# Hybrid streaming encoder step on one Trainium2 core: the SSM's Toeplitz matrix through DRAM, the weight ring filled in two halves, the GELU quarters at later steps

## The chip, the cores and the metric

The kernel runs on one core of one Trainium2 chip. The metric is the time of one execution on the device in microseconds (us), lower being better. One execution was also recorded by the hardware profiler; all rows below come from it. The engines are named as in the profile: PE is TensorE's matmul, PEld its weight load, DVE is VectorE, ACT is ScalarE, POOL is GpSimd, SP is SyncE, which issues nearly all transfers (SPq is its queue of instructions).

## The reference, cut to what matters

One layer of a streaming encoder on 1024 prompt and 64 sample positions, 1088 columns in all, model width 1024, everything in fp32.

```
xn = rmsnorm(h, gain);  z = xn @ w_in            # q, k, v, zA, u, zB, gA, gB in one product
attn = sliding-window attention(q, k, v)         # 64-query blocks, sinks, partial rotary
y    = Re(C h) + D u,  h = A h + B u             # SSM: 32 groups of 16 channels, 64 complex states
s    = gelu(y);  s = s * sigmoid(s @ w_glu)
ya = (attn * silu(zA)) @ w_o_attn;  ys = (s * silu(zB)) @ w_o_ssm
h = h + (sigmoid(gA) * ya + sigmoid(gB) * ys) @ w_out
h = h + sigmoid(h @ w_pg) * (p @ w_pp);  y = rmsnorm(h, final_gain)
```

## The kernel before, in words

Activations lie transposed: 128 channels on the partitions, 1088 columns along the free axis, as 43 slots (`S.alloc`) of one such tile each, and four more in the tile `quad`. A free slot is handed out first in, first out, so a transfer into a slot waits for whoever read it last. Every fp32 product is made of three matmuls, L259 to L261 (`mm3`): weight and operand are each split into a rounded high part and the rest, and low times high, high times low and high times high are summed. A split (`split_to`, `hl_split`) is one ACT copy (L1134) and one DVE subtraction (L162).

**Steps.** The program is written as a long row of matmul groups. Each group calls `pump()` twice (once in the stages called `seven`), which counts a clock of steps and runs whatever was planned for that step with `at(step, f)`. So the tables `ROUND_AT`, `OUT_AT`, `BACK_AT`, `RING_AT`, `X_AT` say beside which matmuls the side work is written. The framework then schedules all of it, so an instruction can stand on its engine somewhat ahead of or behind the place where it was written. Each engine runs its own row in order, and each waits on semaphores for what it reads or overwrites.

**SSM rounds.** The SSM runs in eight rounds r of four groups. `s_wb` (step `ROUND_AT[r]`) builds a 128x64 tile `m` and then the Toeplitz matrix `t4` of the round by eight transfers, L736, each of which copies a part of `m`, shifted down by 16 rows per i, from SBUF to SBUF in runs of 16 floats (64 bytes). `s_state` (L765 and a chain of DVE and POOL operations) computes the states, `s_state2` finishes them. `s_out` (step `OUT_AT[r]`) multiplies: L815 uses the Toeplitz matrix, L816 the states; ACT evicts with L817, and L820 writes the result to `y_dram`. `tt_` holds two Toeplitz tiles, used in turn; both are zeroed once by POOL (L719), and the transfers write only the triangle that isn't zero.

**GELU.** When two rounds have written a quarter q of y, `s_back` (step `BACK_AT[q]`, L825) reads it back into `quad`; five steps later `s_gelu` squares it on ACT (L831), then `s_gelu2` makes the polynomial (DVE L835, and one multiplication L182 that `ENG["gelu"]` gives to DVE, DVE, POOL in turn) and a tanh on ACT (L837), and `s_gelu3` the last multiplication on DVE (L168 `quad<-s,quad`). The result is read only by `z_split`, far into the stage `seven(4)`, which begins at step 196.

**The ring.** From step 144 on, weights come through a ring of four pieces: `rload` transfers a raw weight (L173 on SP), `make` splits one half of it into the next piece. `ring_start`, at step `RING_AT` = 142, takes four slots and makes four pieces at once; `RAWS` = 3 is how many raw weights may lie ready.

**The stretch around the change.** Steps 120 to 143 are the product with `w_o_attn` (m = 4 to 7, stage OA here, evicted by ACT L173 into `quad`). Steps 144 to 167 are four gate units m = 4 to 7 of 24 products each (stage M here): blocks of 384, 384 and 320 columns, evicted by DVE (L162 `s<-bank`), then tanh (L1313). Meanwhile the operand sums for the stages `seven` are built from `x` (`x_load` L1274, `x_sums` L1278, the POOL rows of 544 columns, splits of 544 columns). From step 168 on `seven(2)` and then `seven(4)` run Strassen-like products: each piece of the ring serves two sub-blocks of 272 columns, and the bank of one product is copied out by ACT (L173) before the next product may add to it.

Of the kernel before, what the change touches and what calls it, by code (L numbers as in the profile page):

```python
# [12 lines left out]
F32 = mybir.dt.float32  # L13
# [7 lines left out]
P = 128  # L21
# [14 lines left out]
OFF = dict(load=-6, e=-5, wb=0, rot=-1, cf=0, st2=1, gelu=5)  # L36

ENG = dict(tab="VG", e="V", cf="VG", rot="VG", r8="GGGV", unrot="VG", rotadd="VVG", rope="VVVG", ropeadd="GGV", ropec="VG",
           gelu="VVG", norm="VG", w="V", gate="VG", glu="GGGV", mg="VVG", pa="V", h="V", acc="V",
           y="VVVG", z="V", ph="VVG", xs="G", ws="V", rs="VG", ms="V", hq="G", zz="GV", tcp="AV")  # L40
BACK_AT = (152, 158, 164, 170)
ROUND_AT = (32, 40, 50, 73, 86, 103, 121, 140)
OUT_AT = (41, 49, 60, 81, 98, 113, 137, 150)
SLOT = 1096
# [3 lines left out]
BLK2 = [(0, 416), (416, 416), (832, 256)]  # L48
HT = T // 2
RAWS = 3  # L50
RING_AT = 142
RING = 4
X_AT = (148, 151, 154, 158)

# [81 lines left out]
def emit(nc, tc, a, es, dbg=None):  # L136
# [5 lines left out]
    dp = pool(name="dr", bufs=1, space=bass.MemoryType.DRAM)  # L142

    S = Slots(sp, NSLOT)
# [3 lines left out]
    pp_dram = dp.tile([8, P, T], F32, name="pp_dram")  # L148
    pa_dram = dp.tile([8, P, T], F32, name="pa_dram")
    gb_dram = dp.tile([8, P, T], F32, name="gb_dram")  # L150
    zb_dram = dp.tile([4, P, T], F32, name="zb_dram")

    V, G, A, PE, DMA = nc.vector, nc.gpsimd, nc.scalar, nc.tensor, nc.sync
# [85 lines left out]
    def at(i, f, *args):  # L239
        plan.setdefault(i, []).append((f, args))  # L240
# [7 lines left out]
    def later(n, f, *args):  # L248
        at(clock["i"] + n, f, *args)
# [37 lines left out]
    warm = small([P, 256], "warm")  # L287
# [8 lines left out]
    c, cn = BLK[0]  # L296
# [115 lines left out]
    V = Recorder()  # L412
# [227 lines left out]
    V, vtt, stt = V_, vtt_, stt_  # L640
# [71 lines left out]
    def s_wb(r):  # L712

        half(r, "wb")
        sq, e, wb = hget(r, "sq", "e", "wb")
        if r == 0:
            tt_.extend([S.ahalf(), S.ahalf()])
            for x in tt_:
                G.memset(S.hap(x)[:, :512], 0.0)  # L719
        t = S.hap(tt_[r % 2])  # L720
        b = bank[5]
        for x in range(4):
            c = 256 * (x % 2) + P * (x // 2)
            PE.transpose(b[:, P * x:P * x + P], e[:, c:c + P], ident)
        A.activation(wb[:, :512], b, AF.Copy)
        b = bank[7]
        for j in range(2):
            o = b[:, 32 * j:32 * j + 32]
            PE.matmul(o, e[:, P * j:P * j + P], sq[:, SQ_CBR + 32 * j:SQ_CBR + 32 * j + 32], start=True, stop=False)
            PE.matmul(o, e[:, 256 + P * j:256 + P * j + P], sq[:, SQ_NCI + 32 * j:SQ_NCI + 32 * j + 32],  # L730
                      start=False, stop=True)
        m = sq[:, SQ_M:SQ_M + 64]
        vtt(m, b[:, :64], sq[:, SQ_D:SQ_D + 64], ADD)
        t4 = t[:, :512].rearrange("p (g i c) -> p g i c", g=4, i=8)
        for i in range(8):
            DMA.dma_start(t4[0:16 * (i + 1), :, i], m[16 * (7 - i):P].rearrange("p (g c) -> p g c", g=4))  # L736
        hfree(r, "e")

    def s_cf(r):
# [13 lines left out]
    rw, tt_ = {}, []  # L753
# [97 lines left out]
    for r, b in enumerate(ROUND_AT):  # L851
# [5 lines left out]
        if r % 2:  # L857
            q = r // 2
            b = max(BACK_AT[q], OUT_AT[r])
            at(b, s_back, q)  # L860
# [14 lines left out]
    for m in (2, 3):  # L875
        uq[m] = S.alloc()
        w = wget()
# [238 lines left out]
    for mp in range(2):  # L1116
        ts = [gate_unit() for _ in range(2)]
        w = wget()
# [33 lines left out]
    raws, pieces = [], []  # L1152
# [35 lines left out]
    ring = []  # L1188
    rst_ = {}
    ri = {"load": 0, "made": 0, "get": 0}  # L1190

    def rload(n, most=99):
        while ri["load"] < min(n, len(raws)) and len(rst_) < most:
            i = ri["load"]
            rst_[i] = S.alloc()
            first(DMA.dma_start, S.ap(rst_[i])[:, :1024], raws[i])
            ri["load"] += 1

    def make():

        j = ri["made"]
        ri["made"] += 1
        if j >= len(pieces):
            return
        name, i, x, done = pieces[j]
        top = max([i] + ([x] if name[0] == "S" else []))
        rload(top + 1)
        hl = hl_of(ring[j % RING], 512)
        A11, A12 = (S.ap(rst_[i])[:, 512 * y:512 * y + 512] for y in range(2))
        if name[0] == "S":  # L1210
            A21, A22 = (S.ap(rst_[x])[:, 512 * y:512 * y + 512] for y in range(2))
        s1, s2 = (S.ap(ring[-1])[:, 512 * y:512 * y + 512] for y in range(2))
        if name == "S2":
            first(ett, "ws", s1, A21, A22, ADD)
            first(ett, "ws", s2, s1, A11, SUB)
        elif name == "S3":
            first(ett, "ws", A11, A11, A21, SUB)
        elif name == "S4":
            first(ett, "ws", s2, A12, s2, SUB)
        first(hl_split, hl, (A11, A12)[x] if name == "half" else {"S1": s1, "S3": A11}.get(name, s2))  # L1220
        for y in done:
            S.free(rst_.pop(y))
        rload(top + 2, RAWS)

    def pget(n):
        c = ri["get"]
# [14 lines left out]
        pump()  # L1241
        return ps

    def ring_start():
        ring.extend(S.alloc() for _ in range(RING))
        for _ in range(RING):
            make()

    at(RING_AT, ring_start)
    OA = []  # L1250
    for m in range(4, 8):
        if m % 2 == 0:
            w = wget()
# [163 lines left out]
            S.free(GB[x, r])  # L1417

    for k in range(4):
        later(k, x_t1, k)  # L1420
    get = tile_of(ZB)
    seven(2, XP, XSUB, quarters(get, HT, scaled(get), z_late))
    zb, pin = [], []
# [70 lines left out]
    mg, pa = {}, {}  # L1494
# [117 lines left out]
    acc = S.ap(S.alloc())  # L1612
# [35 lines left out]
    for i, (blks, m) in enumerate(steps):  # L1648
        w = pget(2)
        pp_load(i + 1)  # L1650
        pp = S.ap(pq[i])
        for ci in blks:
# [6 lines left out]
            h = h2(m, ci)  # L1659
# [146 lines left out]
```

## Time and profile before

| what | value |
|---|---|
| median of three runs | 881.44 us (879.93 to 883.45) |
| the profiled execution, its own time | 882.6 us |
| its span, first to last instruction | 880.8 us |
| PE busy | 839.0 us (95%) |
| DVE busy | 634.3 us (72%) |
| ACT busy | 359.4 us (41%) |
| POOL busy | 234.4 us (27%) |

PE is busy 95% of the span, so what can be won is the 5% in which it waits and the stretches in which it runs at the lower of its two clock levels. In the profile's 40 slices PE is full nearly everywhere; the slices that are not lie at the start, at 160 to 180 us, at 380 to 400 us, at 420 to 460 us, near 600 and 665 us and at the end. A granted clock (PEclk) of 1.00 is 2.4 GHz, of 0.50 is 1.2 GHz.

### The profile page before, as it was taken

The page shows a single profiled execution, that of the slowest core. Times are in us where ns is not written, and L with a number is a line of the kernel's source. Part 1 is how long each engine was busy: PE and PEld are TensorE (multiplying, and loading weights), DVE is VectorE, ACT ScalarE, POOL GpSimd, SP SyncE. Part 2 cuts the span into 40 slices and gives each one's busy share as a digit, 9 for nine tenths or more (in the row PEclk, how much of TensorE's full clock was granted, in tenths as well). Part 3 has the DMA queues.
Part 4 walks back from the last instruction along what each step waited for, and adds up shares of the span by engine and source line. Part 5 has one row for each costly group of instructions (what it writes and reads, how often), then busy time and mean ns, then how long its engine had stood idle before and what let it go on. Part 6 is the DMA issues. An engine that isn't in the chain of part 4 may idle for free.

```text
span 880.8 us, 14634 instructions
## 1 busy us (share of the span) xinstructions
PE 839.0 (95%) x5571; PEld 801.2 (91%) x5571; DVE 634.3 (72%) x1222; ACT 359.4 (41%) x743; POOL 234.4 (27%) x232
## 2 busy tenths in 40 slices
PE   7999999899999999969979999999999999999994
PEld 6999999677779999969979999999999999999994
DVE  6897699666679758646788766778996556655476
ACT  7312211455543121235444434544447325444552
POOL 4178464111142323127311010140000322100052
PEclk9999999999999999979999999999999999999997
DMA  8431022201002232352342522287254620632124
GB/s 324 153 121 51 21 56 69 72 25 47 12 1 76 55 121 74 93 183 101 125 151 80 191 100 76 91 307 279 76 183 178 238 76 25 225 123 89 60 97 174
DMA packets 59719, 101.26 MB, mean 115 GB/s; under 512 B 23936, under 2 KB 38912, under 8 KB 59648
## 3 DMA queue, kind: packets, MB, share of 16 engines
q1 hardware_dynamic: 59504, 100.31, 33.3%
q8 instruction: 44, 0.72, 0.3%
q14 instruction: 27, 0.22, 0.1%
q10 hardware_dynamic: 144, 0.00, 0.0%
HBM read 74.31 MB, written 24.81 MB: 113 GB/s over the span
## 4 chain that ended last, share of the span: by engine, by line
PE 67%; DVE 14%; DMA 5%; issue 5%; POOL 5%; ACT 3%; SPq 1%; POOLq 0%; DVEq 0%; ACTq 0%
PE bank L259 20%; PE bank L261 19%; PE bank L260 19%; DVE s L162 4%; POOL s L182 4%; DVE s L182 2%; DVE s L168 2%; PE bank L1001 2%; PE bank L1055 2%; PE bank L1043 2%; DVE s L206 1%; DMA quad<-y_dram 1%; POOL quad L182 1%; DMA s<-p 1%; ACT s L204 1%
## 5 line engine op out<-in xcount | busy, mean ns | idle before, releaser
L259 PE MATMUL bank<-s,s 128*128 128x384 f32 (+4 forms) x1568 | 500.5, 320 | 16.5 <-DVE s L168 5.3
L260 PE MATMUL bank<-s,s 128*128 128x384 f32 (+4 forms) x1568 | 494.8, 316 | 0.0
L261 PE MATMUL bank<-s,s 128*128 128x384 f32 (+4 forms) x1568 | 494.6, 316 | 0.0
L259 PEld LDWEIGHTS bank<-s,s 128*128 128x128 f32 x1568 | 297.2, 190 | 25.6 <-issue 6.9
L260 PEld LDWEIGHTS bank<-s,s 128*128 128x128 f32 x1568 | 297.3, 190 | 2.2 <-issue 1.4
L261 PEld LDWEIGHTS bank<-s,s 128*128 128x128 f32 x1568 | 297.3, 190 | 0.6 <-issue 0.2
L162 DVE TENSOR_TENSOR s<-s,s 128x512 fp32r<-128x512 f32 (+3 forms) x172 | 133.2, 786 | 60.0 <-ACT s L1134 54.1
L182 POOL TENSOR_TENSOR s<-s,s 128x272 f32<-128x272 f32 (+5 forms) x73 | 94.3, 1296 | 216.8 <-DVE s L162 95.0
L1134 ACT ACTIVATE s<-s 128x512 fp32r<-128x512 f32 (+1 forms) x150 | 92.9, 631 | 63.0 <-PE bank L261 40.7
L182 DVE TENSOR_TENSOR s<-s,s 128x256 f32<-128x256 f32 (+5 forms) x148 | 93.6, 644 | 15.6 <-ACT s L1667 7.6
L173 ACT ACTIVATE s<-bank 128x272 f32<-128x272 f32 (+4 forms) x111 | 46.5, 428 | 112.4 <-PE bank L261 97.7
L168 DVE SCALAR_TENSOR_TENSOR s<-s,s 128x416 f32<-128x416 f32 (+5 forms) x66 | 44.8, 693 | 37.0 <-ACT s L173 29.4
L162 DVE TENSOR_TENSOR s<-bank,s 128x272 f32<-128x272 f32 (+3 forms) x105 | 46.2, 462 | 32.8 <-PE bank L730 14.4
L204 ACT ACTIVATE s<-s 128x1024 fp32r<-128x1024 f32 (+5 forms) x38 | 35.3, 935 | 69.0 <-PE bank L261 53.1
L182 POOL TENSOR_TENSOR quad<-quad,s 128x272 f32<-128x272 f32 (+1 forms) x14 | 18.0, 1296 | 110.4 <-DMA quad<-x 90.6
L182 POOL TENSOR_TENSOR s<-s 128x256 f32<-128x256 f32 (+3 forms) x26 | 25.2, 973 | 68.3 <-DVE s L162 24.8
L206 DVE TENSOR_TENSOR s<-s,s 128x1024 fp32r<-128x1024 f32 (+3 forms) x30 | 34.5, 1161 | 4.6 <-ACT s L204 4.6
L1010 ACT ACTIVATE s<-bank,at 128x192 f32<-128x192 f32 (+2 forms) x68 | 27.0, 409 | 23.9 <-DVE at L168 23.9
L165 POOL TENSOR_TENSOR rst<-rsw,mhalf 128x3 f32<-128x3 f32 (+4 forms) x7 | 6.0, 872 | 111.8 <-DVE rsw L363 111.8
L1134 ACT ACTIVATE s<-quad 128x544 fp32r<-128x544 f32 x36 | 23.1, 656 | 28.4 <-DVE quad L182 27.8
L182 POOL TENSOR_TENSOR s<-s,at 128x768 f32<-128x768 f32 (+1 forms) x8 | 14.8, 1853 | 52.2 <-DVE at L1019 35.9
L162 DVE TENSOR_TENSOR s<-quad,s 128x544 fp32r<-128x544 f32 x36 | 26.0, 744 | 1.2 <-ACT s L1134 1.2
(145 smaller groups left out, 776.7 us busy)
## 6 DMA issues: line engine op xcount, KB each, us to landing
s<-w_in SPq DMA_DIRECT2D x32, 512.0 KB
s<-x SPq DMA_DIRECT2D x19, 544.0 KB
s<-w_pg SPq DMA_DIRECT2D x16, 512.0 KB
pa_dram<-s SPq DMA_DIRECT2D x8, 544.0 KB
gb_dram<-s SPq DMA_DIRECT2D x8, 544.0 KB
quad<-gb_dram SPq DMA_DIRECT2D x8, 544.0 KB
s<-pa_dram SPq DMA_DIRECT2D x8, 544.0 KB
pp_dram<-quad SPq DMA_DIRECT2D x8, 544.0 KB
```

The source lines that it names most:

```text
L162: V.tensor_tensor(o, x, y, op)
L168: V.scalar_tensor_tensor(o, x, s, y, op0, op1)
L173: f(*x, **k)
L182: (nc.gpsimd if eng(key) == "G" else nc.vector).tensor_tensor(o, x, y, op)
L204: A.activation(f32r(h), x, AF.Copy, scale=1.0 if scale is None else scale)
L206: (G if on == "G" else V).tensor_tensor(f32r(l), x, h, SUB)
L259: PE.matmul(ps, f32r(wh), f32r(xl), start=first, stop=False, **k)
L260: PE.matmul(ps, f32r(wlo), f32r(xh), start=False, stop=False, **k)
L261: PE.matmul(ps, f32r(wh), f32r(xh), start=False, stop=last, **k)
L1001: PE.matmul(o, q, KTR[rows, 64 * n + 64 - nk:64 * n + 64], start=True, stop=True)
L1010: A.activation(pe[:, 64 + x * nk:64 + (x + 1) * nk], bank[3 + kv][:, jp * nk:(jp + 1) * nk], AF.Exp, bias=nm[:, x:x + 1], scale=0.125, acc ...
L1134: A.activation(f32r(hl[0]), raw, AF.Copy)
```

## The change

Three things change.

1. The Toeplitz matrix. `s_wb` no longer copies in eight parts from SBUF to SBUF. It writes `m` (128x64) to a DRAM tile `t_dram[r % 2]` of 240 rows, whose last 112 rows are zeroed once from `warm` at round 0, and reads it back with one transfer whose source is shifted by -16 rows per i: 128 partitions x 4 groups x 8 shifts, 4096 runs of 64 bytes. The eight transfers moved 4 x (16 + 32 + ... + 128) = 2304 such runs. The two POOL zeroings go.
2. The ring. `ring_start` runs twice, at steps 136 and 143, with two slots and two pieces each; up to step 143 only one raw weight may lie ready, then three.
3. The GELU. `BACK_AT` moves from 152, 158, 164, 170 to 176, 186, 196, 206, and all four multiplications L182 go to DVE. The four splits `x_t1` come one step later.

```diff
-           gelu="VVG", norm="VG", w="V", gate="VG", glu="GGGV", mg="VVG", pa="V", h="V", acc="V",
+           gelu="V", norm="VG", w="V", gate="VG", glu="GGGV", mg="VVG", pa="V", h="V", acc="V",
-BACK_AT = (152, 158, 164, 170)
+BACK_AT = (176, 186, 196, 206)
...
-RING_AT = 142
+RING_AT = (136, 143)
...
+    t_dram = dp.tile([2, 240, 64], F32, name="t_dram")
...
         if r == 0:
             tt_.extend([S.ahalf(), S.ahalf()])
-            for x in tt_:
-                G.memset(S.hap(x)[:, :512], 0.0)
+            for x in range(2):
+                DMA.dma_start(t_dram[x, P:], warm[:112, :64])
...
         t4 = t[:, :512].rearrange("p (g i c) -> p g i c", g=4, i=8)
-        for i in range(8):
-            DMA.dma_start(t4[0:16 * (i + 1), :, i], m[16 * (7 - i):P].rearrange("p (g c) -> p g c", g=4))
+        m_dram = t_dram[r % 2]
+        DMA.dma_start(m_dram[0:P], m)
+        rows = bass.AP(m_dram.tensor, m_dram.offset + 112 * 64, [[64, P], [16, 4], [-1024, 8], [1, 16]])
+        DMA.dma_start(t4, rows)
         hfree(r, "e")
...
-        rload(top + 2, RAWS)
+        rload(top + 2, ri["raws"])
...
-    def ring_start():
-        ring.extend(S.alloc() for _ in range(RING))
-        for _ in range(RING):
-            make()
-
-    at(RING_AT, ring_start)
+    def ring_start(raws_):
+        ring.extend(S.alloc() for _ in range(2))
+        ri["raws"] = raws_
+        make()
+        make()
+
+    at(RING_AT[0], ring_start, 1)
+    at(RING_AT[1], ring_start, RAWS)
...
     for k in range(4):
-        later(k, x_t1, k)
+        later(k + 1, x_t1, k)
```

**How instructions move.** In the changed file lines behind the new one are numbered one to five higher: L259 to L261 become L260 to L262, L815 and L816 become L818 and L819, L736 becomes L737 (write) and L739 (read), L173 becomes L174, L831 and L837 become L834 and L840. Names such as `s17_134_2664` are a slot and its user; `bank2_66` is a PSUM bank.

TensorE at the end of OA, before. `s17_134` holds the last weight of OA, `s42_168` the ring's first piece:

```order
L260 MATMUL bank2_66<-s17_134_2664,s3_4_82 128x320
L261 MATMUL bank2_66<-s17_134_2664,s2_3_81 128x320
L815 MATMUL bank5_69<-s10_74_1109,s9_75_1110 128x136
L815 MATMUL bank6_70<-s10_74_1109,s9_75_1110 128x136
L816 MATMUL bank5_69<-s11_167_3566,s5_160_3348 128x136
L815 MATMUL bank5_69<-s10_74_1109,s9_75_1110 128x136
L816 MATMUL bank5_69<-s11_167_3566,s5_160_3348 128x136
L816 MATMUL bank6_70<-s11_167_3566,s5_160_3348 128x136
L815 MATMUL bank6_70<-s10_74_1109,s9_75_1110 128x136
L816 MATMUL bank6_70<-s11_167_3566,s5_160_3348 128x136
L259 MATMUL bank0_64<-s21_22_100,s42_168_3610 128x384
```

The same place after (`s16_161` is now the ring's first piece), where stage M follows OA at once:

```order
L260 MATMUL bank2_66<-s40_135_2642,s2_3_82 128x320
L261 MATMUL bank2_66<-s17_134_2641,s3_4_83 128x320
L262 MATMUL bank2_66<-s17_134_2641,s2_3_82 128x320
L260 MATMUL bank0_64<-s21_22_101,s16_161_3449 128x384
L261 MATMUL bank0_64<-s20_21_100,s16_161_3449 128x384
L262 MATMUL bank0_64<-s20_21_100,s16_161_3449 128x384
```

and the last round's product stands 28 products (24 of m = 4 and 4 of m = 5) further down:

```order
L262 MATMUL bank0_64<-s26_27_106,s11_171_3578 128x384
L818 MATMUL bank5_69<-s10_74_1110,s9_75_1111 128x136
L819 MATMUL bank5_69<-s39_46_395,s5_160_3307 128x136
L818 MATMUL bank5_69<-s10_74_1110,s9_75_1111 128x136
L819 MATMUL bank5_69<-s39_46_395,s5_160_3307 128x136
L818 MATMUL bank6_70<-s10_74_1110,s9_75_1111 128x136
L819 MATMUL bank6_70<-s39_46_395,s5_160_3307 128x136
```

All other rounds' products keep their places among the matmuls.

SyncE at the last round, before: the eight parts of the Toeplitz matrix, then a row of `x` and a raw weight.

```order
L820 DMA y_dram_73<-s16_161_3496 8x16x136 x4
L736 DMA s9_75_1110<-s5_160_3348 16x4x16
L736 DMA s9_75_1110<-s5_160_3348 32x4x16
L736 DMA s9_75_1110<-s5_160_3348 48x4x16
L736 DMA s9_75_1110<-s5_160_3348 64x4x16
L736 DMA s9_75_1110<-s5_160_3348 80x4x16
L736 DMA s9_75_1110<-s5_160_3348 96x4x16
L736 DMA s9_75_1110<-s5_160_3348 112x4x16
L736 DMA s9_75_1110<-s5_160_3348 128x4x16
L1274 DMA s15_177_3661<-x 128x1088
L173 DMA s14_174_3624<-w_in 128x1024
```

After: the write and the read of it, with a row of `x` (into slot 15) and a raw weight (into slot 40) between, both of which go into slots that the last block of OA reads.

```order
L823 DMA y_dram_73<-s6_165_3465 8x16x136 x4
L1279 DMA s41_176_3613<-x 128x1088
L737 DMA t_dram_77<-s5_160_3307 128x64
L1279 DMA s15_177_3614<-x 128x1088
L174 DMA s40_184_3695<-w_in 128x1024
L739 DMA s9_75_1111<-t_dram_77 128x32x16
L174 DMA s42_173_3582<-w_in 128x1024
```

ScalarE where stage M ends and `seven(2)` begins, before. The evictions of the first product of `seven(2)` are the last two rows; `s39_209` is the GELU's third quarter:

```order
L831 ACTIVATE s39_209_4123<-quad_63 128x1088
L1134 ACTIVATE s20_21_99<-s12_179_3707 128x544
L1313 ACTIVATE s0_205_3998<-s0_205_3998 128x384
L1134 ACTIVATE s22_23_101<-s12_179_3707 128x544
L1134 ACTIVATE s4_170_3612<-s6_175_3635 128x512
L837 ACTIVATE s39_209_4123<-s39_209_4123 128x1088
L1134 ACTIVATE s24_25_103<-s14_192_3849 128x544
L1134 ACTIVATE s41_171_3613<-s38_198_3885 128x512
L1313 ACTIVATE s0_205_3998<-s0_205_3998 128x320
L1134 ACTIVATE s26_27_105<-s14_192_3849 128x544
L173 ACTIVATE s17_208_4109<-bank4_68 128x272
L173 ACTIVATE s17_208_4109<-bank5_69 128x272
```

After: the first quarter (`s38_212`) begins between those two evictions, and its tanh stands four rows behind them.

```order
L1318 ACTIVATE s0_203_3942<-s0_203_3942 128x320
L174 ACTIVATE s9_205_4044<-bank4_68 128x272
L834 ACTIVATE s38_212_4252<-quad_63 128x1088
L174 ACTIVATE s9_205_4044<-bank5_69 128x272
L1137 ACTIVATE s16_161_3449<-s6_174_3587 128x512
L1137 ACTIVATE s14_162_3450<-s40_204_4027 128x512
L174 ACTIVATE s39_207_4113<-bank4_68 128x272
L840 ACTIVATE s38_212_4252<-s38_212_4252 128x1088
```

The second quarter follows later in `seven(2)`, the third and fourth where `seven(4)` begins.

## Rows read from the trace of the kernel before

**Rows 1.** PE's waits from 376 to 462 us: for whom, total, times, longest.

```profile
PE bank L259 <- ACT s L173: 4.8, 1, 4.8
PE bank L815 <- DMA s<-s: 3.7, 1, 3.7
PE bank L259 <- ACT s L1134: 3.0, 1, 3.0
PE bank L259 <- DVE s L162: 1.9, 1, 1.9
PE bank L816 <- DVE s L803: 0.5, 1, 0.5
```

**Rows 2.** Timeline of PE, 382 to 401 us: start, us, row [idle before <-releaser].

```profile
382.75 0.30 PE L261 MATMUL bank<-s,s 128*128 128x320 f32 x1
386.80 1.19 PE L815 MATMUL bank<-s,s 128*128 128x136 f32 x4 [3.74 <-DMA s<-s]
...
390.91 0.66 PE L816 MATMUL bank<-s,s 128*128 128x136 f32 x2
394.56 1.01 PE L259 MATMUL bank<-s,s 128*128 128x384 f32 x2 [2.99 <-ACT s L1134]
...
400.74 0.34 PE L259 MATMUL bank<-s,s 128*128 128x384 f32 x1
```

**Rows 3.** Stretches: busy us of each engine, granted clock, DMA share, GB/s.

```profile
core 0: us, PE busy (x) PEld busy (x) DVE busy (x) ACT busy (x) POOL busy (x), PEclk, DMA share, GB/s
386.80:400.56 13.76, 10.24 (x34) 9.41 (x35) 4.63 (x11) 7.68 (x11) 5.26 (x4) 0.50 0.91 336
453.31:458.11 4.80, 0.00 (x0) 0.00 (x0) 4.77 (x7) 3.52 (x7) 1.10 (x1) 1.00 0.00 0
458.11:462.76 4.65, 4.65 (x25) 4.65 (x25) 4.65 (x7) 1.27 (x3) 0.00 (x0) 0.63 0.80 248
447.14:489.88 42.74, 37.94 (x291) 37.72 (x290) 37.25 (x55) 22.47 (x41) 6.33 (x3) 0.96 0.30 103
```

**Rows 4.** Timeline of PE at round 6's product.

```profile
372.47 0.40 PE L815 MATMUL bank<-s,s 128*128 128x136 f32 x2
...
374.24 0.43 PE L259 MATMUL bank<-s,s 128*128 128x384 f32 x1
```

**Rows 5.** Timeline of PE: two starts of units in stage M.

```profile
409.30 0.34 PE L259 MATMUL bank<-s,s 128*128 128x384 f32 x1
...
421.20 0.34 PE L259 MATMUL bank<-s,s 128*128 128x384 f32 x1
```

**Rows 6.** Timelines of POOL and ACT: the third quarter's multiplication, its tanh, the eviction.

```profile
451.49 2.93 POOL L182 TENSOR_TENSOR s<-s,quad 128x1088 f32<-128x1088 f32 x1 [19.36 <-DVE s L835]
454.45 1.11 ACT L837 ACTIVATE s<-s 128x1088 f32<-128x1088 f32 x1 [2.05 <-POOL s L182]
...
457.68 0.67 ACT L173 ACTIVATE s<-bank 128x272 f32<-128x272 f32 x2
```

**Rows 7.** Timeline of DVE: the second GELU quarter.

```profile
444.70 0.73 DVE L835 TENSOR_SCALAR s<-s 128x1088 f32<-128x1088 f32 x1 [2.66 <-ACT s L831]
445.94 1.29 DVE L182 TENSOR_TENSOR s<-s,quad 128x1088 f32<-128x1088 f32 x1
448.41 1.29 DVE L168 SCALAR_TENSOR_TENSOR quad<-s,quad 128x1088 f32<-128x1088 f32 x1
```

**Rows 8.** Timeline of SP: the Toeplitz transfers of rounds 3 and 7.

```profile
275.20 5.46 SPq L736 DMA_DIRECT2D s<-s  x8
...
379.20 5.93 SPq L736 DMA_DIRECT2D s<-s  x8
```

**Rows 9.** Timeline of PE: the product of round 3.

```profile
289.83 0.39 PE L815 MATMUL bank<-s,s 128*128 128x136 f32 x2
```

**Rows 10.** The chain of work that ended last: start, us, what.

```profile
156.27 2.34 DMA y_dram<-s
```

**Rows 11.** The DMA queues from 379 to 387 us.

```profile
q1 hardware_dynamic: 2445, 0.20, 22.0%
```

## Prediction, made before the changed kernel ran

> **What bounds the kernel now.** I read the page's busy table first: PE works 839.0 of 880.8 us, so a change wins only what PE waits or runs at its lower clock. The list of PE's waits then tells which of the 41.8 us lie in the stretch that the diff touches, from 376 to 462 us: five waits, 4.8, 3.7, 3.0, 1.9 and 0.5 [rows 1]. The reader should see who ends each: a Toeplitz transfer (L815 <- DMA), the states (L816 <- DVE), the ring's first pieces (L259 <- ACT L1134), a piece's subtraction (L259 <- DVE L162) and a copy-out (L259 <- ACT L173). The timeline puts three of them between OA's last matmul, which ends at 382.75 + 0.30 = 383.05, and stage M's first at 394.56 [rows 2]. The stretches add what no wait shows: from 386.80 to 400.56 the granted clock is 0.50, the 1.2 GHz level, right behind the idle 3.74 us, and from 458.11 to 462.76 it is 0.63, behind the idle 4.80 us [rows 3].
>
> **Part 1, end of OA: round 7's product and the ring's start.** In the new order PE goes from OA straight into M and the product stands 28 products later. It removes the three waits: 3.74 + 0.53 + 2.99 = 7.26 us. It also keeps the clock up. Round 7's product ran from 386.80 to 390.91 + 0.66 = 391.57, 4.77 us with the 0.53 in it [rows 2]; round 6's took 372.47 to 374.24 plus about 0.25 for its last matmul, 2.02 [rows 4]. Lost to the clock: 4.77 - 0.53 - 2.02 = 2.22. In M, 19 starts took 400.74 - 394.56 = 6.18 us [rows 2]; a unit of M takes 421.20 - 409.30 = 11.90 us for 24 x 1088 columns [rows 5], so 384 columns take 0.175 and 19 of them 3.33. Lost: 2.85. Together 12.33 us.
>
> What must be ready for it: the ring's pieces 0 to 3 are made from steps 136 and 143 on, one raw weight being loaded ahead of time. I take no wait for M's start, since two pieces stand in ACT's and DVE's rows ahead of OA's end; if they came late, the price is in the third rival. The pieces of m = 6 need ring slots that come free when m = 4 is done, at 383.05 + 11.90 = 395, and are needed at 407, two units of 11.90 after M's start: cover of 12 us. The moved product is then due at 383.05 + 11.90 + 4/24 of 11.90 = 396.9.
>
> **Part 2, the Toeplitz matrix through DRAM.** Removed are eight transfers, whose issue alone held SP 5.46 to 5.93 us a round [rows 8]; two issues take their place. SP isn't what PE waits for elsewhere, so I count that as nothing. POOL's two zeroings give way to two small transfers at round 0, both long before any product: nothing. Added is a write, then a read that must wait for the write to land, and behind it on SP what was behind the eight before. The trace has no such read. Bounds: a write to DRAM took 2.34 us [rows 10]; the eight old transfers took from 379.20 [rows 8] to 386.80 [rows 2], 7.6 us for 2304 runs of 64 bytes, and scaled to 4096 runs that is 13.5 us. Below, the read might be as short as the write, 2.34. So the latency of the new pair is 4.7 to 15.9 us, where 7.6 stood. I take 6 to 8: in 379 to 387 us 2445 packets took 22.0% of 16 engines [rows 11], 0.22 x 16 x 8 us / 2445 = 11.5 ns each, so 4096 of them take 4096 x 11.5 / 16 = 2.9 us when spread over all engines, and 2.34 + 2.9 + about 1 of waiting is nearer to the lower end.
>
> A page speaks against this part: the Trainium skill, "DMA: Bandwidth & Descriptors", section "Why small descriptors are slow (HBM only)", says that SBUF to SBUF transfers are spared the penalty of small descriptors, and its "Specifications" want at least 512 bytes for full rate. The new read is just the kind that pays. An estimate by that page, each run priced as 512 bytes at its 435 GB/s, is 4096 x 512 / 435 GB/s = 4.8 us, and the sum stays as it is; no row of before shows a 64-byte read from DRAM.
>
> Who needs it and when: round 7's transfers were issued at 379.20. The read stands behind a row of `x` and a raw weight, both of which go into slots that OA's last block still reads, so it may be issued only at about 383.05. With 2.3 to 13.5 us it lands at 385.4 to 396.6, and 396.9 is when PE wants it: covered, barely so at the upper bound. Of the other rounds, round 3 has 289.83 - 275.20 = 14.6 us from issue to product [rows 8, 9], round 5 reads alike, and the others, read the same way, have at least 15.8. At the upper bound, 15.9, rounds 3 and 5 cost 1.3 us each; at my value nothing.
>
> **Part 3, the GELU.** The second quarter's pieces (0.73, 1.29 and 1.29 us on DVE [rows 7]) crowd the end of M; with them gone the 1.9 us of L259 <- DVE L162 [rows 1] goes, since the delayed subtraction stood behind such rows. The gap of 4.80 us is a chain that the rows spell out: POOL's multiplication took 2.93 us to 454.42, where DVE takes 1.29 [rows 6, 7]; the tanh behind it on ACT began at 454.45 after 2.05 us of waiting; and behind that tanh, in order, stood two splits and the copy-out at 457.68 [rows 6], on which PE waited until 458.11. In the new order the first copy-outs of `seven(2)` stand ahead of any tanh, and POOL has no part in it. Gain 4.80, and the clock: 24 starts in 458.11 to 462.76 took 4.65, at full clock 272 columns take 0.124 by the same unit of M [rows 5], 2.98, so 1.65 to 1.67 more. I take 1.65.
>
> What it costs: all four quarters now fall into `seven(2)` and the start of `seven(4)`. On DVE the third's multiplication, 1.29 us, is new, the rest only moves. On ACT each square or tanh is one activation of 1.11 us [rows 6], and one stands between two copy-outs that PE wants in turn: 0 to 1.11 us at each of the four in `seven(2)`. I take 0.7 in all, near the low end, since ACT was busy in only 22.47 of 42.74 us there [rows 3]. The moved results are read only late in `seven(4)`, 40 steps behind the last quarter, so nobody waits for them.
>
> **Sum.** 12.33 + 1.9 + 4.80 + 1.65 - 0.7 = 20.0 us. The profiled execution took 882.6, 1.16 above the median of 881.44. 882.6 - 20.0 = 862.6; a median of such runs lies at 862.6 - 1.16, about **861.5 us**.
>
> **Rivals.**
>
> *The wait comes back in `seven(2)`.* DVE was busy 37.25 of 42.74 us from 447.14 to 489.88, and 4.77 of the 4.80 us in which PE stood [rows 3]. Without the gap and the low clock PE would want the same work in 42.74 - 4.80 - 1.65 = 36.3 us, and DVE has no room in that unless some of its load (two quarters at 3.31 us were partly in it) lies elsewhere. The ring's four pieces let it fall behind by some 5 us before PE waits. Then a wait as large as the old one returns, 6.45 us: about 868. For it: these rows. Against it: two quarters now come when the first sub-blocks are done, and the other two beyond them.
>
> *M starts late anyway.* Step 136 is early enough only if SP, which waits in order for slots, has the raw weights there; if one arrives late, M stands idle and begins at the lower clock, and half of the 12.33 us stays: 861.5 + 6.2, about 867.7.
>
> *Little is won.* What the stretch gains is lost at a later transfer or at a DVE that is late for its next stage: some 878 to 884.
>
> *Slower: the DRAM read makes the products wait.* If the read of 64-byte runs takes so long that write and read pass each round's slack, every round's product on PE waits for L - slack (14.6, 14.7, 15.8, 15.8, about 18 for round 7, 19 and more for rounds 0, 1 and 2). At L = 19.9 us, a read of over 17 us, that is 5.3 + 5.2 + 4.1 + 4.1 + 1.9 + 0.9, some 21 us, which eats the gain; from about 21 us on, 25 to 30 are lost and the time is 886 to 892. For it: nothing in the trace has this form. Against it: that price is above even the scaled upper bound of 13.5 us, and the new read is a single transfer over 128 partitions, not a row of eight.
>
> By the estimate from that page of the Trainium skill, 4.8 us for the read, the pair would take 2.34 + 4.8 = 7.1 us, and this rival would not occur.
>
> **How the numbers follow.** The forecast has 0.60, the returning wait 0.20, the late M 0.07, little won 0.08, the slow read 0.05. The range takes in the first three: below, the sum without the 0.7, with a few us for waits elsewhere that SP's shorter row may spare and the spread of the runs of before (1.5 below the median): 857.5. Above, the two rivals at 868 and the 2 x 1.3 us of rounds 3 and 5: 870. A measurement of this kernel tells about 0.5%, 4.4 us, from no change, so faster means below 877.0: 0.60 + 0.20 + 0.07 and a little of the fourth, 0.88; same 0.07, slower 0.05.
>
> **What would show it.** In the new profile: no idle PE at 383 and L818 near 397; PEclk 1.00 throughout 380 to 465; the Toeplitz read landing before L818 in every round, 6 to 8 us after the write's issue; no L260 <- ACT L174 wait where `seven(2)` starts, which should be near 433 instead of 447; and all that follows 20 us earlier. Wrong would make it: a DMA releaser before L818 in rounds 3, 5 or 7, a wait of several us on L174 or a piece in `seven(2)`, or waits near 600 and 665 us that grow by what was won.

## The result, and the profile after

The changed kernel takes 866.89 us (866.03 to 869.12, four runs) where the kernel before, run beside it, takes 881.71 us: a ratio of 0.9836 with a 95% interval of 0.9809 to 0.9863, 14.8 us faster. Forecast were 861.5 us in a range of 857.5 to 870. The profiled execution of the changed kernel took 866.03 us, its span 864.2, so between the two traces lie 880.8 - 864.2 = 16.6 us. Of the ten executions of e1_t below, the profiled one (921.84 us, granted clock 0.84 where the others had 0.97 and more) is left out of its numbers, and its trace is not read.

The list of PE's waits after, from 370 to 470 us: for whom, total, times, longest. It answers to [rows 1]:

```profile
PE bank L260 <- DVE s L163: 4.1, 2, 3.5
```

The row holds two waits, 3.51 and 0.60 us. Four of the five waits of before are gone. The fifth, 1.95 us before the first matmul of m = 7, has shrunk to the 0.60; the 3.51 us are new. The timeline of PE, where OA ends (384.62 is its last matmul) and where stage M waits:

```profile
384.62 0.30 PE L262 MATMUL bank<-s,s 128*128 128x320 f32 x1
384.77 0.34 PE L260 MATMUL bank<-s,s 128*128 128x384 f32 x1
...
398.79 0.39 PE L818 MATMUL bank<-s,s 128*128 128x136 f32 x2
...
410.76 0.41 PE L260 MATMUL bank<-s,s 128*128 128x384 f32 x1
...
418.71 0.44 PE L260 MATMUL bank<-s,s 128*128 128x384 f32 x1 [3.51 <-DVE s L163]
...
428.87 0.41 PE L260 MATMUL bank<-s,s 128*128 128x384 f32 x1 [0.60 <-DVE s L163]
```

Against [rows 2]: M follows OA 0.15 us behind, and round 7's product (L818) starts at 398.79 without a wait. Inside M, PE stands 3.51 us before the second block of m = 6, and 0.60 before m = 7, the place of the old 1.95. The stretches (busy us of each engine, granted clock, DMA share, GB/s), against [rows 3]:

```profile
core 0: us, PE busy (x) PEld busy (x) DVE busy (x) ACT busy (x) POOL busy (x), PEclk, DMA share, GB/s
384.98:414.80 29.82, 29.70 (x183) 29.46 (x182) 21.93 (x26) 15.47 (x24) 18.73 (x14) 1.00 0.65 203
418.66:422.00 3.34, 3.29 (x13) 3.29 (x14) 2.09 (x2) 1.71 (x3) 3.26 (x3) 0.66 0.42 155
430.00:470.00 40.00, 40.00 (x300) 40.00 (x300) 31.06 (x50) 20.67 (x38) 2.92 (x2) 1.00 0.41 145
```

The clock stays at 1.00, the 2.4 GHz level, from OA through 414.80; it falls to 0.66 on average behind the new wait; and `seven(2)`, from 440.86 on, runs without a stop. The starts of the same matmul in both kernels tell where the 16.6 us come from:

| TensorE's matmul | before | after | after less before | change since the row above | forecast for it |
|---|---|---|---|---|---|
| OA's last | 382.75 | 384.62 | +1.87 | +1.87 | 0 |
| m = 6, first | 421.20 | 410.76 | -10.44 | -12.31 | -12.33 |
| m = 7, first | 435.20 | 428.87 | -6.33 | +4.11 | -1.9 |
| the copy-out's waiter in `seven(2)` | 458.11 | 446.87 | -11.24 | -4.91 | -4.80 |
| 36 matmuls on | 464.25 | 451.38 | -12.87 | -1.63 | -1.65 |
| the waiter at 606 us | 606.86 | 592.56 | -14.30 | -1.43 | 0 |
| the waiter at 668 us | 668.50 | 652.68 | -15.82 | -1.52 | 0 |
| the last | 873.49 | 856.77 | -16.72 | -0.90 | 0 |

So the forecast's gains at the end of OA and at `seven(2)` came to within 0.1 us, and three things came that it did not hold: 6.0 us worse at m = 6 (4.11 + 1.9), 2.9 us better at 606 and 668 us, and 1.87 us worse ahead of the stretch. From the first matmul of m = 6 to that of m = 7 PE took 428.87 - 410.76 = 18.11 us where a unit without a wait takes 11.90: 4.11 us are the two waits, and the other 2.1 go mostly to the lower clock behind the first (an estimate: the mean clock from 418.66 to 430.00 is 0.85, which costs 1.7 us). At 606 and 668 us stood two waits of before, 2.0 us together, that are gone; where the other 0.9 us came from was not traced. PE's waits of before, 480 to 700 us (after there is none):

```profile
PE bank L259 <- ACT quad L173: 1.2, 1, 1.2
PE bank L259 <- DVE s L168: 0.8, 1, 0.8
```

**Where the new wait comes from.** The sums of `x` are built in four turns, k = 0 to 3. The timelines of SP, POOL, ACT and DVE in the changed kernel, against the new wait's end at 418.71. First SP:

```profile
381.07 0.33 SPq L737 DMA_DIRECT2D t_dram<-s  x1
...
385.09 0.63 SPq L739 DMA_DIRECT2D s<-t_dram  x1
394.51 0.33 SPq L174 DMA_DIRECT2D s<-w_in  x1
394.89 2.68 SPq L1279 DMA_DIRECT2D s<-x  x4
```

then POOL and ACT, then DVE:

```profile
400.72 1.36 POOL L183 TENSOR_TENSOR s<-s 128x544 f32<-128x544 f32 x1 [7.03 <-ACT s L1283]
...
412.95 3.16 POOL L183 TENSOR_TENSOR s<-s,s 128x544 f32<-128x544 f32 x2
416.14 1.20 ACT L1137 ACTIVATE s<-s 128x544 fp32r<-128x544 f32 x2 [3.50 <-POOL s L183]
```

```profile
389.34 5.11 DVE L163 TENSOR_TENSOR s<-s 64x272 f32<-64x272 f32 x4 [0.66 <-POOL s L183]
...
410.07 0.55 DVE L163 TENSOR_TENSOR s<-bank,s 128x384 f32<-128x384 f32 x1
...
416.83 1.36 DVE L163 TENSOR_TENSOR s<-s,s 128x544 fp32r<-128x544 f32 x2 [3.37 <-ACT s L1137]
418.11 0.55 DVE L163 TENSOR_TENSOR s<-bank,s 128x384 f32<-128x384 f32 x1
```

Read from the end: PE may use its bank again at 418.71 because DVE evicted it at 418.11 to 418.66. The eviction had been possible since about 407, when PE had left that block of m = 5. It stood in DVE's row behind two splits of the sums of `x`, which waited for ACT's copies, which waited for POOL's sums, which ended at 416.1. POOL was late because it had stood 7.03 us for rows of `x`; and these were issued only from 394.89, because the raw weight ahead of them on SP waited for a slot that round 7's state held until DVE's four subtractions ended at 394.45. M had moved 12 us ahead; round 7's state and the loads behind it had not. This is the order of events in one trace; what happens when one link is taken out, g_slot below shows.

### The profile page after: what moved, and what is told of

Same layout as the page of the kernel before. It is cut to its first block, busy times and chain, and to the rows that moved or that the text cites. A ratio compares the mean times of both kernels' runs of the same rounds, so it can differ in the third digit from the quotient of the medians.

```text
span 864.2 us, 14545 instructions
## 1 busy us (share of the span) xinstructions
PE 834.3 (97%) x5571; PEld 798.5 (92%) x5571; DVE 632.9 (73%) x1223; ACT 359.8 (42%) x743; POOL 230.2 (27%) x229
## 4 chain that ended last, share of the span: by engine, by line
PE 76%; DVE 10%; POOL 5%; issue 4%; ACT 3%; DMA 2%; SPq 1%; POOLq 0%; DVEq 0%; ACTq 0%
PE bank L260 23%; PE bank L262 22%; PE bank L261 22%; POOL s L183 4%; DVE s L163 3%; PE bank L1004 2%; DVE s L183 2%; PE bank L1058 2%; PE bank L1046 2%; DVE s L207 1%; POOL quad L183 1%; DVE s L169 1%; ACT s L205 1%; DMA s<-w_in 1%; PE bank L768 1%
## 5 line engine op out<-in xcount | busy, mean ns | idle before, releaser
L260 PE MATMUL bank<-s,s 128*128 128x384 f32 (+4 forms) x1568 | 499.3, 319 | 8.3 <-DVE s L163 4.1
L262 PE MATMUL bank<-s,s 128*128 128x384 f32 (+4 forms) x1568 | 494.4, 315 | 0.0
L261 PE MATMUL bank<-s,s 128*128 128x384 f32 (+4 forms) x1568 | 493.9, 315 | 0.0
L260 PEld LDWEIGHTS bank<-s,s 128*128 128x128 f32 x1568 | 296.9, 190 | 16.3 <-issue 5.3
L261 PEld LDWEIGHTS bank<-s,s 128*128 128x128 f32 x1568 | 296.8, 189 | 2.0 <-issue 1.4
L262 PEld LDWEIGHTS bank<-s,s 128*128 128x128 f32 x1568 | 296.8, 189 | 0.8 <-issue 0.4
L163 DVE TENSOR_TENSOR s<-s,s 128x512 fp32r<-128x512 f32 (+3 forms) x172 | 127.4, 749 | 64.4 <-ACT s L1137 58.2
L174 ACT ACTIVATE s<-bank 128x272 f32<-128x272 f32 (+4 forms) x111 | 46.9, 429 | 109.3 <-PE bank L262 100.6
L183 POOL TENSOR_TENSOR s<-s,at 128x768 f32<-128x768 f32 (+1 forms) x8 | 14.8, 1848 | 52.2 <-DVE at L1022 35.9
```

Source lines behind the costliest of these rows:

```text
L163: V.tensor_tensor(o, x, y, op)
L174: f(*x, **k)
L183: (nc.gpsimd if eng(key) == "G" else nc.vector).tensor_tensor(o, x, y, op)
L260: PE.matmul(ps, f32r(wh), f32r(xl), start=first, stop=False, **k)
L261: PE.matmul(ps, f32r(wlo), f32r(xh), start=False, stop=False, **k)
L262: PE.matmul(ps, f32r(wh), f32r(xh), start=False, stop=last, **k)
```

## The experiments

**One part alone.** The kernel before with one of the three parts.

The Toeplitz path alone:

```diff
-        for i in range(8):
-            DMA.dma_start(t4[0:16 * (i + 1), :, i], m[16 * (7 - i):P].rearrange("p (g c) -> p g c", g=4))
+        DMA.dma_start(m_dram[0:P], m)
...
+        DMA.dma_start(t4, rows)
```

> Only the Toeplitz path through DRAM is changed, ring and GELU as before. Theory A (the ring's two halves and the GELU carry the gain, the DRAM path almost none): TensorE's order is as before, with round 7's product still ahead of stage M, so its wait for the Toeplitz matrix stays between 3 and 6 us and the time is 880 to 884 us, within 0.3% of before. Theory B (the DRAM path is what removes the wait of 3.7 us, and with it the lower clock behind it): that wait is under 1 us, stage M begins some 6 us earlier, and the time is 873 to 877 us.

880.38 us, ratio 0.9962 (0.9943 to 0.9981): in A's range of times, far above B's; but the gain of 0.38%, some 3 us, is a little more than A's 0.3%. Whether the wait for the Toeplitz matrix stayed, as A said, is read from e5_no_ring below.

The ring alone:

```diff
-RING_AT = 142
+RING_AT = (136, 143)
```

> Only the ring is changed. Theory A: the ring alone moves round 7's product behind 28 products of stage M and removes the three waits of 7.3 us and the lower clock, 12.3 us; the new wait of 3.5 us in stage M with 1.6 us at the lower clock comes with it, and the 4.8 us at the start of seven(2) stay: 872 to 876 us. Theory B: without the DRAM path the eighth Toeplitz transfer, which now stands behind a raw weight on SyncE, is late for the moved product, PE waits 2 to 5 us for it, and the time is 876 to 881 us.

877.43 us, ratio 0.9936 (0.9914 to 0.9959). In TensorE's row the product stands behind the 28 products of M, as in the changed kernel, and PE's waits from 376 to 480 us are

```profile
PE bank L259 <- DVE s L162: 6.4, 3, 5.1
PE bank L259 <- ACT s L173: 4.1, 1, 4.1
```

No wait for a DMA: the ring by itself moves the product and removes the three waits at the end of OA, and the eight old transfers are in time for it. So theory B falls, though the time lies in its range. What A missed is the size of the wait inside M, 5.1 us and not 3.5, which fits a time above 876.

The GELU alone:

```diff
-BACK_AT = (152, 158, 164, 170)
+BACK_AT = (176, 186, 196, 206)
```

(with `gelu="V"` and the later `x_t1`.)

> Only the GELU quarters and the four splits are moved. Theory A: the 4.8 us wait at the start of seven(2) and its 1.65 us at the lower clock go, perhaps the 1.9 us in stage M too; the waits at the end of OA stay: 872 to 876 us. If the waits near 606 and 667 us go as well, the GELU is their cause and the time is 870 to 873; if they stay, the ring or the DRAM path is. Theory B (the gap at seven(2) comes from stage M being late, not from the GELU): 879 to 883 us.

877.2 us, ratio 0.9943 (0.9919 to 0.9968), 1.2 us above A's range. The waits from 376 to 480 us:

```profile
PE bank L815 <- DMA s<-s: 4.3, 1, 4.3
PE bank L259 <- DVE s L162: 3.5, 3, 1.5
PE bank L259 <- ACT s L1134: 3.1, 1, 3.1
```

The copy-out's wait of 4.8 us is gone with M where it was, so the GELU's quarters at their old steps were its cause (the splits `x_t1` moved with them in this run and were not tried apart). The 1.9 us of DVE in M aren't gone: there are now three such waits of 3.5 us together. Near 606 and 668 us PE still waits 0.8 and 0.4 us.

**Two parts of three.** The changed kernel with the eight transfers put back:

> The changed kernel with the eight SBUF to SBUF transfers put back. Theory A: no DMA wait before round 7's product, the same new wait of 3 to 5 us in stage M, and the time of the changed kernel within 2 us: 865 to 869 us. Theory B: PE waits 2 to 5 us for the last of the eight transfers, and the time is 870 to 876 us.

871.56 us, ratio 0.9872 (0.9824 to 0.9919). The waits from 376 to 480 us:

```profile
PE bank L259 <- DVE s L162: 5.8, 2, 5.0
```

No DMA wait, so B falls again, though the time lies in its range; but the wait inside M is 5.0 us where the changed kernel has 3.5. There the DRAM path pays some 1.5 us. Through which link isn't shown. SP here, with OA's last matmul at 387.96:

```profile
390.66 0.62 SPq L1276 DMA_DIRECT2D s<-x  x1
394.49 0.33 SPq L173 DMA_DIRECT2D s<-w_in  x1
394.87 0.91 SPq L1276 DMA_DIRECT2D s<-x  x2
```

The row of `x` behind the eight transfers is issued 2.7 us behind that matmul, in the changed kernel 1.0 ahead of it (383.65). But the raw weight and the next rows of `x` come 6.5 and 6.9 us behind it here and 9.9 and 10.3 in the changed kernel. So the loads that stand in the chain above came sooner here, and yet the wait is the longer one.

The changed kernel with the ring filled at once at step 142:

> The changed kernel with the ring filled at once at step 142, as before; the DRAM path and the GELU stay changed. Theory A (the ring alone moves round 7's product, and the DRAM path saves some 3 us only where rows of x are late): the product is again ahead of stage M with its waits for the Toeplitz matrix and the ring's pieces, some 6 to 7 us idle in 383 to 395, and the time is 872 to 877 us. Theory B (the DRAM path shortens the wait): less than 4 us idle there, and 868 to 872 us.

875.38 us, ratio 0.9926 (0.9898 to 0.9954), theory A, and PE's waits from 376 to 480 us:

```profile
PE bank L818 <- DMA s<-t_dram: 5.1, 1, 5.1
PE bank L260 <- ACT s L1137: 2.2, 1, 2.2
PE bank L260 <- DVE s L163: 1.8, 1, 1.8
```

With the product in its old place PE waits 5.1 us for the read from DRAM, longer than the 3.7 of before. From the write's issue (381.71) to the product (390.67) pass 9.0 us, where 7.6 stood: the new path doesn't hasten the last round's matrix at all. That the waits at the end of OA are gone is the ring's doing.

**The GELU's third multiplication back on POOL.**

```diff
-           gelu="V", norm="VG", ...
+           gelu="VVG", norm="VG", ...
```

> The changed kernel with the third quarter's multiplication on GpSimd again, as before. Theory A (at the later steps nobody waits for it; the gap at seven(2) went because the quarters moved): the time of the changed kernel within 1.5 us. Theory D (the multiplication's 2.9 us on GpSimd were the cause by themselves): a wait of 1 us or more behind it where seven(4) begins, 868 to 872 us.

867.45 us, ratio 0.9838 (0.9809 to 0.9868): theory A. At the later steps PE has no wait behind POOL's slower multiplication, so the move of the quarters is enough without the change of engine. Whether the change of engine at the old steps would have been enough too was not run.

**The changed kernel again, and five tries on the new wait.**

> The changed kernel once more, beside the two below on the same chip. Theory A (the wait in stage M comes from SyncE's row: a raw weight waits there for a slot of round 7's state, and rows of x behind it): the wait of about 3.5 us before the 24th product of m = 6 is there again, and the time is 864 to 869 us, ratio 0.981 to 0.986. Theory B (that wait was a disturbance of one run): no such wait, or one elsewhere.

866.4 us, ratio 0.9825 (0.9796 to 0.9854), with 3.48 us of waiting at the same matmul: no chance event.

The third raw weight two steps later and into another slot:

```diff
-    at(RING_AT[1], ring_start, RAWS)
+    at(RING_AT[1], ring_start, 0)
+
+    def third_raw():
+        S.free_list.append(S.free_list.pop(0))
+        x_load(0)
+        ri["raws"] = RAWS
+        rload(3, RAWS)
+
+    at(X_AT[0] - 3, third_raw)
```

> The changed kernel, with the third raw weight of the ring loaded two steps later and into another slot, one that the last product with w_o_attn frees, and not into the slot of round 7's state. Theory A: SyncE issues the rows of x some 6 to 9 us earlier against TensorE's work, VectorE's row has no late split ahead of the evictions, the wait of 3.5 us and the 1.5 us at the lower clock behind it go: 860 to 863 us, about 5 us faster than the changed kernel. Theory C (GpSimd's sums, not the loads, are late: 16 rows of 1.4 to 1.7 us each for four k): the wait shrinks by less than half, and the time is 864 to 867 us.

868.26 us, ratio 0.9845 (0.981 to 0.988): by the wait theory C, and the time 1.3 us above its range. SP did issue the rows of `x` from 385.20 on, 9.7 us sooner, and yet:

```profile
385.20 3.24 SPq L1287 DMA_DIRECT2D s<-x  x3
...
388.34 1.79 DVE L163 TENSOR_TENSOR s<-s 64x272 f32<-64x272 f32 x4 [0.66 <-POOL s L183]
...
390.44 0.55 DVE L163 TENSOR_TENSOR s<-bank,s 128x384 f32<-128x384 f32 x1
...
391.08 0.53 ACT L1327 ACTIVATE s<-s 128x384 f32<-128x384 f32 x1 [6.14 <-issue]
...
392.78 4.26 POOL L183 TENSOR_TENSOR s<-s,s 128x544 f32<-128x544 f32 x3 [4.47 <-ACT s L1291]
...
416.33 0.55 DVE L163 TENSOR_TENSOR s<-bank,s 128x384 f32<-128x384 f32 x1
```

(rows of SP, DVE, ACT, POOL and DVE). The eviction came at 416.33, and PE waited 3.02 us and then 1.35 at m = 7. ACT's scaling of the second row of `x` stood behind a tanh (391.08) that waited for M's first eviction (390.44), and that behind round 7's state on DVE (388.34); so the loads were one link of the chain, not the one that bound it.

Other places for the sums of `x` (`X_AT`) and for round 7 (`ROUND_AT`), each on top of this kernel. First the sums much later:

```diff
-X_AT = (148, 151, 154, 158)
+X_AT = (148, 153, 159, 164)
```

> As g_slot, and the sums of x for k = 1, 2, 3 planned at steps 153, 159, 164 (151, 154, 158 before), so that in VectorE's row all three evictions of m = 5 stand ahead of the splits of the sums of k = 2. Theory E (the wait of 3.0 to 3.5 us in stage M is an eviction that stands behind splits which wait for GpSimd's sums, in VectorE's order): the wait before the second block of m = 6 is under 1 us, and the time is 860 to 864 us, unless seven(2) then waits for the sums of k = 3. Theory F (VectorE and GpSimd have too much work in stage M, in whatever order): a wait of 3 us or more appears in m = 7 or at the start of seven(2), and the time is 865 to 869 us.

871.42 us, ratio 0.9869 (0.9854 to 0.9884), above both theories' ranges. The wait at the second block of m = 6 is gone, as theory E said, and 1.96 us in the third block and 4.56 us at m = 7 stand in its place, as theory F said. The sums a little later:

```diff
-X_AT = (148, 151, 154, 158)
+X_AT = (148, 152, 157, 162)
```

> As g_slot, with the sums of k = 1, 2, 3 at steps 152, 157, 162. In VectorE's row one split of k = 2 stands ahead of the second eviction of m = 5, two behind it. Theory E: a wait of 1 to 2 us is left there, and the time is 862 to 866 us. Theory F: as with the other order, 865 to 869 us.

867.45 us, ratio 0.9821 (0.9806 to 0.9835), in theory F's range: one wait is left in M, 3.15 us at m = 7. Again an eviction behind splits, and POOL's row names who holds them, the output tile of round 7 that a transfer to `y_dram` still reads:

```profile
417.11 2.69 POOL L183 TENSOR_TENSOR s<-s 128x544 f32<-128x544 f32 x2 [5.56 <-DMA y_dram<-s]
```

That tile handed out last, and nothing else:

```diff
+    def y_last():
+        S.free_list.remove(5)
+        S.free_list.append(5)
+
+    at(X_AT[2] - 2, y_last)
```

> As i2_slot_x, with one slot more moved: the output tile of round 7's product, which SyncE still reads for y_dram until some 416 us, is handed out last, so that GpSimd's sums of k = 2 go into the slot of a Toeplitz matrix instead. Theory H (each wait in stage M is a chain through a slot or a queue that round 7 leaves late; here GpSimd stood still 5.6 us for that transfer, and VectorE's eviction behind it): GpSimd's sums of k = 2 begin some 5 us earlier, the wait of 3.15 us at m = 7 is under 1 us, and the time is 862 to 865 us. Theory F (too much work in stage M in whatever order): the wait returns at another place with 3 us or more, 866 to 869 us.

867.88 us, ratio 0.982 (0.9775 to 0.9865), in theory F's range. POOL's sums of k = 2 begin at 406.19, 11 us sooner, and the wait at m = 7 is gone; but now the rows of `x` for k = 3 come late (issued at 417.09), POOL stands

```profile
424.46 1.37 POOL L183 TENSOR_TENSOR s<-s 128x544 f32<-128x544 f32 x1 [11.09 <-ACT s L1297]
```

and PE waits 5.27 us inside m = 7, with 1.26 and 0.52 us in m = 6. Last, round 7 earlier, on top of g_slot:

```diff
-ROUND_AT = (32, 40, 50, 73, 86, 103, 121, 140)
+ROUND_AT = (32, 40, 50, 73, 86, 103, 121, 138)
```

> As g_slot, with round 7 planned at step 138 and not 140, so that its states on VectorE and GpSimd are done some 4 us earlier; the sums of x as in the changed kernel. Theory G (the chain begins with round 7's states: they hold up stage M's first eviction, and with it the tanh, the scaling of x and GpSimd's sums): the wait in stage M shrinks to under 1.5 us, 861 to 865 us. Theory E: the order of evictions and splits is the same, so the wait stays at 2 to 3.5 us, 865 to 868 us.

868.86 us, ratio 0.9844 (0.9823 to 0.9864), above both ranges: the wait at m = 6 shrinks from 3.02 to 0.76 us, as theory G said, and the one at m = 7 grows from 1.35 to 3.58. So in g_slot round 7's date was the link behind most of the wait at m = 6.

In all five, 3 to 7 us of waiting in M were left or came back. From OA's last matmul to the first of `seven(2)` PE is 8.2 us faster than before in the changed kernel, 8.3 in g_slot, 3.3 in j1, 10.0 in i2_slot_x, 4.0 in k1 and 8.3 in i6_round_slot. So i2_slot_x did win some 1.9 us there, which its time doesn't show clear of the intervals. Theory F said that the wait would come back elsewhere, and in j1, i2_slot_x and k1 it did; but its reason, too much work, isn't in the counts: in k1, from 383 to 433 us,

```profile
383.00:433.00 50.00, 43.39 (x263) 42.51 (x262) 33.65 (x42) 23.34 (x35) 26.52 (x19) 1.00 0.57 177
```

DVE is busy 33.65 of 50 us and POOL 26.52, which leaves room on average. Where the chain was followed (the changed kernel, g_slot, i2_slot_x, k1), each wait had its own, through engines that work in order, slots and SP's row; that an order without a wait exists was neither found nor excluded, and no version beat the changed kernel beyond the intervals.

## Why the prediction was right, and where it was not

*The bound and the end of OA.* Right in size: 12.31 us against 12.33, the lower clock counted in. M follows OA without a wait, so the rival of the late M did not come. What the prediction left open is who does it. It worked the change out as one; the runs show the ring alone moving the product and removing the three waits.

*The Toeplitz path.* The pair was put at 4.7 to 15.9 us, taken as 6 to 8. In round 5 the write is issued at 331.32 and the read at 332.78, and the read moves its bytes within 333.90 to 336.50:

```profile
331.32 0.33 SPq L737 DMA_DIRECT2D t_dram<-s  x1
332.78 0.63 SPq L739 DMA_DIRECT2D s<-t_dram  x1
```

```profile
333.90:336.50 2.60, 2.60 (x17) 2.60 (x16) 1.93 (x6) 0.00 (x0) 1.45 (x2) 1.00 1.08 101
```

That is 5.2 us for the pair, with all 16 DMA engines busy while the read moves. But round 5 is the best of the eight. By the records of the 64-byte packets the pair took 5.3 to 8.1 us in six other rounds and 10.0 in round 7, from the write at 381.07 to the last packet at 391.1; there the read was issued only at 385.09, as the prediction had it, behind the slots that OA's last block frees. So 6 to 8 us were too narrow on both sides, and the bounds of 4.7 to 15.9 held. The read moved its bytes in 2.3 to 4.2 us; the 2.9 worked out from 11.5 ns a packet were near. No product waited for it in the changed kernel (round 7's stood at 398.79, 7.7 us behind), so the rival of the slow read falls, and so does that of little won. The prediction's estimate of 4.8 us for the read, from the Trainium skill's page "DMA: Bandwidth & Descriptors" (its sections "Specifications" and "Why small descriptors are slow (HBM only)"), is more than any round took; the trace decides. The step that failed is "SP isn't what PE waits for elsewhere, so I count that as nothing": alone the path gains 0.38% (0.19 to 0.57), some 3 us, and without it the wait in M is 5.0 and not 3.5 us. Whether SP's shorter row is what gains them, and where the rest of the 3 us lies, was not shown.

*The GELU.* Right: 4.91 + 1.63 us against 4.80 + 1.65, and `seven(2)` has no wait, so the rival of the returning wait did not come, nor the 0.7 us taken for the new rows on ACT. That the multiplication left POOL was worth nothing measurable at the later steps (f_pool).

*The 1.9 us in M, and the new 3.5.* Wrong, and the largest miss, 6.0 us. It begins with a misreading of a row of before. The prediction took the 1.9 us for a wait for a piece's subtraction. The rows of DVE and PE at that place, before:

```profile
430.83 3.75 DVE L162 TENSOR_TENSOR s<-s,s 128x512 fp32r<-128x512 f32 x4
434.51 0.55 DVE L162 TENSOR_TENSOR s<-bank,s 128x384 f32<-128x384 f32 x1
```

```profile
435.20 0.41 PE L259 MATMUL bank<-s,s 128*128 128x384 f32 x1 [1.95 <-DVE s L162]
```

L162 is the line of every subtraction. The one that ended last ahead of PE, at 435.06, has a bank as its source: it is M's own eviction, standing behind four splits. So the kernel before already had a wait of the kind that then grew. GELU rows did stand ahead of it, as the prediction said; but with them gone (e3_gelu) the waits in M are 3.5 us and not none. The failing step is the paragraph on what must be ready for M: it followed the ring's pieces and their slots and stopped there. It did not follow M's own evictions, which stand in DVE's row behind side work; the sums of `x` had a date in steps, and the steps had moved 12 us ahead of round 7 and of the loads. The rival *M starts late anyway* had the place nearly right (side work late for M, by SP's waits for slots) and a price of 6.2 us, but put it at M's start and on the pieces.

*Not foreseen.* The waits at 606 and 668 us are gone, 2.9 us. The ring alone keeps 0.5 us of them, the GELU alone 0.8 and 0.4, both without the DRAM path (e4_no_t) 0.7; e5_no_ring has none. But f_pool and j1, which have all three parts, have 0.5 and 1.2. So which part of the change ends them was not settled. The 1.87 us ahead of the stretch are in the last section.

The three ratios alone multiply to 0.9962 x 0.9936 x 0.9943 = 0.9842, and the whole has 0.9836: within the intervals the parts add up. The forecast of 20.0 us against 14.8 is thus the sum's +6.0 at m = 6, less 2.9 at 606 and 668, less the 0.7 not needed, plus 1.9 ahead of the stretch: 4.3, less 0.9 at the tail, 3.4 between the two traces. The profiled execution stood 0.9 us above the median before and 0.9 below it after, which makes 5.2 between the medians. That the time lies in the range is in part luck: the range's upper end stood for other rivals, and the 6.0 us lost at m = 6, which nothing in the prediction priced, were partly paid back by the 2.9 us at 606 and 668, which nothing in it priced either.

## What to carry to other kernels

When a stage starts sooner, list all that must be ready inside it and not only at its start: the side work whose date is tied to the stage moves ahead with it, while what that work needs (the round before, a slot, a row in the load queue) does not. An eviction that shares an in-order engine with splits of other data is only as early as the latest input of those splits. When a row of waits names a line that a helper shares, look up which instruction of that line ended the wait: here it was an eviction and not a piece. And where several parts change at once, run each alone before telling which of them did it.

## What the runs showed of the hardware

**The same instructions at another clock.** The stretch from 160 to 240 us has the same TensorE row in all kernels here. In the kernel before its clock is

```profile
160.00:240.00 80.00, 76.59 (x492) 56.70 (x493) 55.88 (x138) 41.89 (x164) 15.02 (x11) 1.00 0.12 34
```

and in e4_no_t, on another run,

```profile
160.00:240.00 80.00, 77.29 (x454) 57.18 (x454) 53.53 (x131) 39.02 (x152) 13.57 (x10) 0.91 0.12 34
```

with 38 fewer matmuls in the same time. TensorE's row in e4_no_t is that of before up to 356 us; so the 5.2 us by which its last matmul of OA comes later, all lost between 160 and 200 us, are not its doing. Nor are the changed kernel's 1.87 us: they arise between 40 and 60 us, ahead of the first write to `t_dram` at 113 us, and at 60 us e2_ring, without the DRAM path, is 1.4 us later than before, j1, with it, 0.2 sooner. Over the profiles read here the last matmul of OA lay between 0.04 us sooner and 5.2 us later than before. Two traces are therefore best compared by differences from a matmul just ahead of the change, as in the table above.

**DVE beside POOL.** The last four subtractions of round 7's state (64x272) took DVE 5.11 us in the changed kernel, while POOL ran four rows at 388.34 to 393.69, and 1.79 us in g_slot, where POOL stood idle from 388.31 to 392.78. One by one: three of the four took 1.5 to 1.6 us each beside rows of POOL, the fourth, from 394.01 on and behind POOL's last row, 0.44, as all four did in g_slot. In the changed kernel SP's raw weight waited these 3.3 us longer. They don't make the wait in M: e2_ring and e4_no_t have 1.79 us there, too, and PE waits 5.1 and 5.0 us.
